# A third quarter's attention outputs kept on the chip: added by GpSimd, with an adding transfer for the first output, and columns in other places of the dense stage

## The chip, the cores and the metric

The kernel runs on one core of one Trainium2 chip. The metric is the device time of one execution in microseconds (us), the median of several runs. The engines are called by their work: TensorE (PE in the profile), VectorE (DVE), ScalarE (ACT), GpSimd (POOL) and SyncE (SP), which only issues transfers here.

## What is computed

One layer of a streaming encoder over 2048 frames of width 1024, in float32: an attention over chunks with a learned position bias, then a dense SwiGLU feed-forward network (FFN), each between two RMS norms and with a residual.

```python
def reference(x, ...):                      # DEPTH is 1, so only mixer 0 runs
    h = rms_norm(x, g_pre_mix)
    m = chunk_relpos_attention(h, w_qkv, w_o, rel_bias)
    x = x + rms_norm(m, g_post_mix)
    h = rms_norm(x, g_pre_ffn)
    return x + rms_norm(swiglu(h, w_gate, w_up, w_down), g_post_ffn)

# chunk_relpos_attention: 16 heads of 64; each chunk c of 64 frames sees chunks max(0, c-8)..c
sc = q_blk @ k[k0:k1].T * scale + bias
out = softmax(sc) @ v[k0:k1]                # all heads side by side, then @ w_o
```

## The kernel before, in words

All activations stand transposed, as 128 partitions by eight column tiles by 512 frames. The 2048 frames are four quarters of 512 frames, and two groups of two quarters. Each float32 operand of a dense product is split in two parts, a high one rounded to fp32r (ScalarE, `split`, L360) and a low one, the rest (VectorE, L361); a product is three matmuls, high by high, high by low and low by high (`products`, L201 to L203). Weights are split in the same way (L136, L137). Many dense products follow Strassen's scheme with seven block products (`B11`, `B21`, `T1`, `T2`, `B22`, `T3`, `T4`), whose operands are sums and differences of blocks; those of the weights that are sums are made by transfers that copy and then add in DRAM (`weight_sums`, L1042 and L1046) or on VectorE (L1109).

The stages follow one another: the projections to queries, keys and values (0 to about 470 us), the attention (to about 1054 us), the dense stage `o_rest` that finishes the output projection of the last two quarters (to about 1110 us), then the FFN, gate and up products and the down product, for each group.

*The attention* goes through the quarters in the order 1, 0, 2, 3 (`SEQ_OF`), so the third quarter in time is quarter 2. A quarter has eight jobs, one for each pair of heads, of four steps each. A step `t` transposes its block of softmax scores on TensorE (L586, into one of a ring of three score banks), lets GpSimd scale the scores of a later step by the inverse row sum (`scaled`, L571), starts the scores of the step three ahead (L542, L543, then VectorE adds the bias in L552 and ScalarE takes the exponential in L557), and fills TensorE's remaining time with dense products of the quarter before (`fill`). When a job ends, `output` multiplies with the values (L622); the result is in a score bank, and ScalarE copies its high part into `ats` (L635), VectorE its low part (L643). For quarter 2 a second copy `at` (L639) goes through a tile of the ring `io` to `at_d` in DRAM. The ring `io` has three tiles, which outputs (`y`), residuals (`res`) and these copies share. For the last quarter only one copy is kept, unsplit (L630).

Dense work during a quarter: `o_quarter` projects the first two quarters' outputs, and during the fourth quarter `o_first` makes the first of the seven block products of the last two quarters, in two halves of four output tiles each. The first half's sum is kept in `p1_d`; the second half's, added to it, is the first four output tiles of quarter 2 in `o_d`. Beside it `Columns` prepares the other operands: it takes quarter 2's attention output back into `at2` (from `at_d`, in two loads), and `t1` (L707) and `others` (L712 to L716) form differences with quarter 3's output. `Late` norms a finished quarter: it loads output and residual, multiplies on VectorE (L1401), adds the residual (L1404, on GpSimd during the attention) and stores `x1`.

*Order.* TensorE's instructions are issued in the order of the program. The other engines' are ordered by a scheduler, by priority and by when it expects them to be ready. Work beside a dense product is put on the list `later`, where each step has a cost; `tick` takes steps off it as TensorE's work is written. The unit is one product of three 512-column matmuls. `timed` places steps at given units, and `pause` waits for some. A name's place (slot) is one of seven tiles `hb0` to `hb6`, which attention outputs, columns, raw loads and terms share one after another; `Blocks` has a list of slots for each group:

```python
self.slot = dict(zip(("B21", "B22", "T3", "T4", "B11", "T1", "T2"), slots))
loads = {"L11": ("T3", 1, 0, 0), "L12": ("T3", 0, 1, 0), "L21": ("T4", 1, 0, 4), "L22": ("T4", 0, 1, 4)}
```

`L11` and the other loads bring blocks of `x1` into the places of T3 and T4; `B11` to `T4` are columns built from them by norm (L877), sum and split. SP's transfers all have line L72, and they are issued in the order of SP's queue.

Of the kernel before, what the change touches and what calls it, by code (L numbers as in the profile page):

```python
# [9 lines left out]
F32 = mybir.dt.float32  # L10
F32R = mybir.dt.float32r  # L11
I32 = mybir.dt.int32  # L12
AF = mybir.ActivationFunctionType
ALU = mybir.AluOpType
# [3 lines left out]
P = 128  # L18
# [5 lines left out]
KT = D // P  # L24
HALF = 512
# [24 lines left out]
def trunk(  # L50
# [45 lines left out]
    y_d = [dram.tile([P, KT, HALF], F32, name=f"y_{i}") for i in range(2)]  # L96

    a_d = [{n: dram.tile([P, NF // 2, HALF], F32, name=f"a{n}_{g}") for n in BLOCKS} for g in range(NG)]
    at_d = dram.tile([P, KT, HALF], F32, name="at")
    p1_d = dram.tile([P, 4, HALF], F32, name="p1")  # L100
    sum_o = {n: [dram.tile([P, 1024], F32, name=f"o_{n}_{c}") for c in range(2)] for n in ("S1", "S2", "S3", "S4")}
    sum_d = {n: dram.tile([NF // 2, P, HALF], F32, name=f"d_{n}") for n in ("S1", "S2", "S3", "S4")}
# [52 lines left out]
    def part_split(c):  # L155
        n = len(ready) - (c > 0)
        if n == len(raws):
            return
        if c == 0:
            ready.append([w_tile(f"{n}_{i}") for i in range(2)])  # L160
        split_part(*ready[n][c], raws[n][c])
# [45 lines left out]
    later = deque()  # L207
# [29 lines left out]
    def pause(w):  # L237
        return [(w, lambda: None)]
# [14 lines left out]
    def io(name):  # L253
        return xp.tile([P, HALF], F32, tag="io", name=name, bufs=3)
# [214 lines left out]
    class Attend:  # L469
# [139 lines left out]
        def output(self):  # L609
            n, p = self.n, self.p  # L610
            v = values[n, p // 2]
            terms = [(0, 4, 0, HALF)]
            for r in range(1, 5 if self.prev else 4):
                if self.prev:
                    terms.append((r, r - 1, 0, r * P))
                if r < 4:
                    terms.append((r, 4 + r, r * P, HALF))
            po = ring[1] if self.alone else self.bank("po")
            for m, (r, kb, c0, c1) in enumerate(terms):
                for h in range(2):  # L620
                    c = (p % 2) * P + h * 64
                    pe.matmul(  # L622
                        po[heads[h], c0:c1], v[:, kb, c : c + 64], self.pT[:, h, r, c0:c1],
                        start=m == 0, stop=m == len(terms) - 1,
                    )
            if n == SEQ_OF[-1]:
                if p == 0:
                    ats[n] = hb_tile(2, F32, (KT, HALF))
                with tc.high_priority(offset=400):
                    act.activation(ats[n][:, p, :], po, AF.Copy)  # L630
                return lambda: None
            if p == 0:
                ats[n] = Cols(((0, 1), (2, 3))[SEQ_OF.index(n) % 2])
            with tc.high_priority(offset=400):
                act.activation(ats[n].hi(p), po, AF.Copy)  # L635
            if n == SEQ_OF[-2]:
                t = io("at")
                with tc.high_priority(offset=400):
                    act.activation(t, po, AF.Copy)  # L639
                sp.dma_start(at_d[:, p, :], t)  # L640
            def low():
                with tc.high_priority(offset=400):
                    dve.tensor_tensor(ats[n].lo(p), po, ats[n].hi(p).bitcast(F32), op=ALU.subtract)  # L643

            return low
# [22 lines left out]
    def o_first(src):  # L668

        for half in range(2):  # L670
            w = take()
            for d in range(4):
                pt = dense_bank(d)
                if half:
                    p1 = io("p1")
                    sp.dma_start(p1, p1_d[:, d, :])
                for k in range(4):
                    hi, lo = w.tiles[d // 2]
                    c = slice(k * 256 + d % 2 * P, k * 256 + d % 2 * P + P)
                    products(pt, hi[:, c], lo[:, c], src.hi(4 * half + k), src.lo(4 * half + k), k == 0, k == 3)  # L680
                    yield 3 * C512
                    if (d, k) == (2, 3):
                        part_split(0)
                    elif (d, k) == (3, 2):
                        part_split(1)
                if half:
                    dve.tensor_tensor(p1, p1, pt, op=ALU.add)
                    sp.dma_start(o_d[SEQ_OF[-2]][:, d, :], p1)
                else:
                    t = io("y")  # L690
                    act.activation(t, pt, AF.Copy)
                    sp.dma_start(p1_d[:, d, :], t)

    class Columns:

# [3 lines left out]
            self.at3 = None  # L699
            self.t = {}  # L700

        def load(self, half):
            here = slice(4 * half, 4 * half + 4)
            sp.dma_start(self.at2[:, here, :], at_d[:, here, :])

        def t1(self, k):
            dve.tensor_tensor(self.at2[:, k, :], ats[SEQ_OF[-1]][:, k, :], self.at2[:, k, :], op=ALU.subtract)  # L707
# [39 lines left out]
            for c, src in enumerate(both)  # L747
        ]

    def o_rest(cols):  # L750

        first, second = SEQ_OF[-2:]
        roots = [bank("prs").rearrange("p (a b) -> p a b", a=4) for _ in range(2)]
# [54 lines left out]
        def put(name):  # L808
            return [(0.8, lambda k=k: cols.put(name, k)) for k in range(4)]

        later.extend(
            put("T2") + put("T4") + [(0.0, begin)] + blocks[0].spreads(lambda name: roots.pop(0))
            + put("T3") + put("B22") + [(0.0, second_terms)]
        )
        slab = take().tiles
        back.ahead(-4)
        yield from product(banks_y, "T1", True, slab, lambda d: None)
        while "two" not in terms:
            later.popleft()[1]()
        banks_x.extend(bank("pd") for _ in range(4))  # L820
        yield from product(banks_x, "T2", True, None, after_t2)
        yield from product(banks_x, "T3", False, None, after_t3)
# [818 lines left out]
    def ffn():  # L1641

        for g in range(NG):
            i = 2 * g
            if g == 0:
                later.extend(pause(12.0))
                for n in (NQ - 2, NQ - 1):
                    later.extend(lates[n].sums(5.0) + lates[n].rstd(1.5) + lates[n].write(10.0))
                later.extend(pause(16.0) + blocks[1].sums(10.0, True))
            else:  # L1650
                for late in halves:
                    later.extend(late.sums(10.0) + late.rstd(1.5) + late.write(14.0))
# [84 lines left out]
    def open_ffn(n):  # L1737
# [2 lines left out]
        phase["psf"] = stack_f[n].enter_context(tc.tile_pool(name=f"psf{n}", bufs=2, space=PSUM, reuse_waits="tile"))  # L1740

    blocks = [
        Blocks([x1_d[2 * g + t] for t in range(2)], PRE_FFN, ((5, 3, 0, 1, 4, 2, 6), (5, 2, 6, 3, 1, 0, 4))[g])
        for g in range(NG)
    ]
    front, items = None, []
# [29 lines left out]
    for c in project():  # L1776
        tick(c / (3 * C512))
        done += c / (3 * C512)
        if 350.0 < done and done % 8.0 < 1.0:
            next(sums_, None)  # L1780
    drain()
    lates = [Late(o_d[n], POST_MIX, x[n], x1_d[n], n) for n in range(NQ)]
# [25 lines left out]
    for t in range(slots):  # L1808
        share = left[0] / max(per - t % per - 1, 1)
        if t > 0 and t % 4 == 0:  # L1810
            fill(0.5 * share)
            low = jobs[t // 4 - 1].output()
            if t % per == 0:
                low()
                low = lambda: None
                n = t // per - 1
                fill(1e9)
                drain()
                work, left[0] = o_quarter(SEQ_OF[n]), KT * KT * 3 * C512
                if n == NQ - 2:  # L1820
                    work, left[0] = o_first(ats[SEQ_OF[n]]), left[0] / 2
                    cols = Columns()
                    cols.load(0)
                if n > 0:
                    late = lates[SEQ_OF[n - 1]]
                    later.extend(pause(5.0) + late.rows(4.0) + late.write(3.0, pool, 1))
                    later.extend(blocks[0].sums(2.0, which=[SEQ_OF[n - 1]]))
        if t == 16:
            fetch()
        elif t in (20, 22):  # L1830
            part_split(t // 2 - 10)
        job = jobs[t // 4]
        if cols is not None:
            s = t % per
            if s == 6:
                cols.load(1)
            if s in (5, 9, 13, 17):
                cols.t1(s // 4 - 1)
            elif s in (18, 19, 22, 23):
                cols.put("T1", (18, 19, 22, 23).index(s))  # L1840
            elif s in (21, 25, 29):
                cols.others(s // 4 - 5, (0,))
            elif s in (26, 27, 30):
                cols.others((26, 27, 30).index(s), (1, 2))
            tick(1.0)
        job.transposed(t % 4)
        job.fifth()
        if t + AHEAD - 1 < slots:
            jobs[(t + AHEAD - 1) // 4].scaled()
        ahead(t + AHEAD)  # L1850
        if t > 0 and t % 4 == 0:
            low()
        fill(share if t % 4 < 3 else 0.5 * share)
# [7 lines left out]

    open_ffn(1)
    first = lambda part, w: blocks[0].build(part, w, lambda t, k, x_: blocks[0].norm(x_, t, k))
    work, done = o_rest(cols), 0.0
    for c in work:
        if done == 0.0:
            later.extend(timed(
                (2.0, first("L11", 0.0)), (2.0, first("L12", 0.0)), (18.0, first("L21", 0.0)), (18.0, first("L22", 0.0)),
                (33.0, first("B11", 2.5)), (49.0, first("B21", 2.5)), (58.0, first("T1", 2.0)),
            ))  # L1870
        tick(c / (3 * C512))
        done += 1.0
    drain()
    later.extend(timed(
        (0.5, first("T2", 3.0)), (13.0, first("B22", 2.0)), (22.0, first("T4", 2.0)), (31.0, first("T3", 1.0)),
# [77 lines left out]
```

## Time and profile before

| What | Value |
|---|---|
| median of 3 runs (lowest to highest) | 2413.51 us (2412.27 to 2416.07) |
| the profiled execution, its own time | 2407.26 us |
| its span, first to last instruction | 2405.5 us |
| TensorE busy | 2321.7 us, 97% of the span |
| VectorE, ScalarE, GpSimd busy | 1673.5, 1146.9, 328.3 us |
| mean granted clock of TensorE | 0.987 |
| transfers | 550.69 MB, mean 229 GB/s |

In a row of the timeline stand the start, the length, the engine, the line, the operation, what it writes and reads, and in brackets the engine's idle time before it with what ended that. In a group (`x58`) stand the summed busy time, the mean of one in ns, and the idle time before them. The tables by stretches have each engine's busy time.

### The profile page before, as it was taken

What the parts mean: (1) busy time and instruction counts of PE and PEld (TensorE: products, weight loads), DVE (VectorE), ACT (ScalarE), POOL (GpSimd) and SP (SyncE); (2) the same over time, 40 slices, a digit from 0 to 9 for tenths busy, and PEclk for the clock granted to TensorE, in tenths of its full rate; (3) what the DMA queues carried; (4) which work ended last, traced back from release to release, by engine and by line L of the source; (5) the groups of instructions that cost most, each with busy time, mean ns of one, the idle gap of its engine ahead of it and who ended that gap; (6) DMA issues with size and microseconds to landing.
All of it is one profiled execution on the core that took longest, in us unless ns stands there. A gap on an engine that the chain in (4) does not pass through costs nothing.

```text
span 2405.5 us, 32939 instructions
## 1 busy us (share of the span) xinstructions
PE 2321.7 (97%) x11388; PEld 1897.5 (79%) x11388; DVE 1673.5 (70%) x2692; ACT 1146.9 (48%) x1995; POOL 328.3 (14%) x432
## 2 busy tenths in 40 slices
PE   9999999989999899799999999999999999999998
PEld 7788888877777687577778788888888888888887
DVE  8787856666665566579869687777657666555577
ACT  7544543367666576455323343365433333334454
POOL 2000011144333434310110000000000000000001
PEclk9999999999999899899999999999999999999999
DMA  8777999998897897865896654477666657447664
GB/s 307 245 259 257 269 324 277 278 253 220 227 252 239 240 258 238 249 243 178 256 294 218 237 193 170 156 242 246 235 203 205 210 156 249 147 148 251 193 192 145
DMA packets 238310, 550.69 MB, mean 229 GB/s; under 512 B 27296, under 2 KB 43696, under 8 KB 233024
## 3 DMA queue, kind: packets, MB, share of 16 engines
q1 hardware_dynamic: 225344, 497.20, 64.8%
q0 software_dynamic: 12800, 51.39, 7.7%
q8 instruction: 90, 1.47, 0.3%
q14 instruction: 76, 0.62, 0.1%
HBM read 397.96 MB, written 181.98 MB: 241 GB/s over the span
## 4 chain that ended last, share of the span: by engine, by line
PE 59%; DMA 6%; DVE 6%; issue 2%; ACT 1%; SPq 1%; POOL 0%; DVEq 0%; POOLq 0%; ACTq 0%
PE pd L201 6%; PE pd L203 6%; PE pd L202 6%; PE pb L201 4%; PE pb L202 4%; PE pb L203 4%; PE pa L202 3%; PE pa L201 3%; PE tt L622 3%; PE pa L203 3%; PE pc L202 3%; PE pc L201 3%; PE pc L203 3%; PE tt L586 2%; PE st L542 2%
## 5 line engine op out<-in xcount | busy, mean ns | idle before, releaser
L571 POOL TENSOR_SCALAR sc<-sc,rows 128x640 f32<-128x640 f32 (+4 forms) x256 | 196.9, 784 | 318.1 <-DVE rows L567 244.6
L557 ACT ACTIVATE sc<-sc,rows 128x640 f32<-128x640 f32 (+4 forms) x256 | 193.2, 757 | 88.6 <-DVE rows L552 87.1
L201 PE MATMUL pb<-hb,w_wg_T 128*128 128x512 f32 x528 | 208.0, 394 | 10.4 <-DVE terms L1217 7.6
L552 DVE CUSTOM_DVE_ANT_0 sc<-st,bias 128x640 f32<-128x640 f32 (+2 forms) x248 | 174.2, 734 | 52.4 <-PE st L543 30.8
L202 PE MATMUL pb<-hb,w_wg_T 128*128 128x512 f32 x528 | 207.5, 393 | 2.9 <-DVE hb L361 2.9
L203 PE MATMUL pb<-hb,w_wg_T 128*128 128x512 f32 x528 | 207.3, 393 | 0.0
L542 PE MATMUL st<-k,q 128*128 128x384 f32 (+3 forms) x432 | 140.9, 343 | 22.4 <-DVE rows L552 13.3
L586 PEld LDWEIGHTS tt<-ident,sc 128*128 128x128 f32 x928 | 107.2, 143 | 52.5 <-POOL sc L571 20.5
L586 PE MATMUL tt<-ident,sc 128*128 128x128 f32 x928 | 128.6, 279 | 19.8 <-DVE hb L643 9.3
L203 PE MATMUL pd<-a,w_d_T 128*128 128x512 f32 (+1 forms) x368 | 139.8, 380 | 0.1
L201 PE MATMUL pd<-a,w_d_T 128*128 128x512 f32 (+1 forms) x368 | 139.9, 380 | 0.0
L202 PE MATMUL pd<-a,w_d_T 128*128 128x512 f32 (+1 forms) x368 | 139.7, 380 | 0.0
L201 PE MATMUL pa<-hb,w_wg_B 128*128 128x512 f32 x352 | 136.9, 389 | 0.0
L202 PE MATMUL pa<-hb,w_wg_B 128*128 128x512 f32 x352 | 136.9, 389 | 0.0
L203 PE MATMUL pa<-hb,w_wg_B 128*128 128x512 f32 x352 | 136.9, 389 | 0.0
L590 DVE COPY pT<-tt 128x512 f32<-128x512 f32 (+3 forms) x128 | 81.7, 638 | 78.4 <-PE tt L586 77.0
L1219 ACT ACTIVATE terms<-terms 128x512 f32<-128x512 f32 x65 | 41.1, 632 | 184.2 <-DVE terms L1217 184.2
L136 ACT ACTIVATE w_wg_T<-raw 128x1024 fp32r<-128x1024 f32 x88 | 93.0, 1058 | 74.7 <-PE pb L203 34.1
L201 PEld LDWEIGHTS pb<-hb,w_wg_T 128*128 128x128 f32 x528 | 100.3, 190 | 34.3 <-issue 9.3
L543 PE MATMUL st<-k,q 128*128 128x384 f32 (+3 forms) x432 | 127.3, 315 | 0.0
L361 DVE TENSOR_TENSOR a<-raw_a,a 128x512 fp32r<-128x512 f32 x154 | 105.4, 693 | 26.3 <-ACT a L360 26.2
L293 POOL TENSOR_TENSOR rs<-ms,neg_half 128x4 f32<-128x4 f32 (+1 forms) x5 | 5.4, 1088 | 850.0 <-DMA raw_a<-aB 813.7
(313 smaller groups left out, 6227.3 us busy)
## 6 DMA issues: line engine op xcount, KB each, us to landing
raw<-in_w_gu SPq DMA_DIRECT2D x77, 512.0 KB, 4.2
q<-q SPq DMA_DIRECT2D x62, 512.0 KB, 6.6
k<-k SPq DMA_DIRECT2D x54, 512.0 KB, 8.8
s_g_S<-raw POOLq DMA_DIRECT2D x44, 512.0 KB, 3.8
raw_a<-aT SPq DMA_DIRECT2D x88, 256.0 KB, 3.6
raw_d<-d_S SPq DMA_DIRECT2D x88, 256.0 KB, 3.7
raw<-s_g_S SPq DMA_DIRECT2D x44, 512.0 KB, 4.0
bias<-ext_d SPq DMA_DIRECT2D x124, 144.0 KB, 8.7
```

Of the source, the lines that this page charges most:

```text
L136: act.activation(hi, raw, AF.Copy)
L201: pe.matmul(pt, a_hi, b_hi, start=first, stop=False, skip_group_check=go_on)
L202: pe.matmul(pt, a_hi, b_lo, start=False, stop=False, skip_group_check=go_on)
L203: pe.matmul(pt, a_lo, b_hi, start=False, stop=last, skip_group_check=go_on)
L361: eng.tensor_tensor(lo, src, hi.bitcast(F32), op=ALU.subtract)
L542: pe.matmul(st[:, a:b], q[:, 2 * h, cols], kk[:, h, key], start=True, stop=False)
L543: pe.matmul(st[:, a:b], q[:, 2 * h + 1, cols], kk[:, h, key], start=False, stop=True)
L552: dve.tensor_tensor_reduce(out=sc[:, :n], in0=st[:, c0 : c0 + n], in1=rev, scale=-1.0, scalar=3.0e38, op0=ALU.add, op1=ALU.min, accum_out= ...
L557: act.activation(sc[:, :n], sc[:, :n], AF.Exp, bias=nmax, scale=-1.0, accum_out=rows[:, h : h + 1])
L571: last_pool[0] = pool.tensor_scalar(sc[:, :n], sc[:, :n], rows[:, 2 + h : 3 + h], 1.0, op0=ALU.mult, op1=ALU.mult)
L586: pe.transpose(tt[:, u, :], sc[h][:, b * P : b * P + P], ident)
L590: dve.tensor_copy(dst, tt[:, : len(part), :])
```

## The change

In the third quarter in time the second copy `at` and its store are gone, and so are `at_d` and the two loads from it. Instead GpSimd adds the high and low parts of that quarter's output into `at2`, one of eight tiles at every second step of the first half of the fourth quarter (`whole`). In `o_first` both halves copy their bank with ScalarE; the first half stores to `p1_d` and to `o_d`, the second half adds to `o_d` by a transfer issued by GpSimd. In `o_rest` the steps are placed at given units together with the loads and columns of the first FFN group, the places of the columns are others, and the loop that ran the remaining steps by force is gone. In the FFN the norms of the last two quarters begin later, and the weight sums begin earlier in the projections.

```diff
             with tc.high_priority(offset=400):
                 act.activation(ats[n].hi(p), po, AF.Copy)
-            if n == SEQ_OF[-2]:
-                t = io("at")
-                with tc.high_priority(offset=400):
-                    act.activation(t, po, AF.Copy)
-                sp.dma_start(at_d[:, p, :], t)
...
                 pt = dense_bank(d)
-                if half:
-                    p1 = io("p1")
-                    sp.dma_start(p1, p1_d[:, d, :])
...
+                t = io("y")
+                act.activation(t, pt, AF.Copy)
                 if half:
-                    dve.tensor_tensor(p1, p1, pt, op=ALU.add)
-                    sp.dma_start(o_d[SEQ_OF[-2]][:, d, :], p1)
+                    last_pool[0] = pool.dma_start(o_d[SEQ_OF[-2]][:, d, :], t, accum_op=ALU.add)
                 else:
-                    t = io("y")
-                    act.activation(t, pt, AF.Copy)
                     sp.dma_start(p1_d[:, d, :], t)
+                    sp.dma_start(o_d[SEQ_OF[-2]][:, d, :], t)
...
-        def load(self, half):
-            here = slice(4 * half, 4 * half + 4)
-            sp.dma_start(self.at2[:, here, :], at_d[:, here, :])
+        def whole(self, k):
+            first = ats[SEQ_OF[-2]]
+            pool.tensor_tensor(self.at2[:, k, :], first.hi(k).bitcast(F32), first.lo(k).bitcast(F32), op=ALU.add)
...
-        later.extend(
-            put("T2") + put("T4") + [(0.0, begin)] + blocks[0].spreads(lambda name: roots.pop(0))
-            + put("T3") + put("B22") + [(0.0, second_terms)]
-        )
+        later.extend(timed(
+            (0.0, put("T2")), (4.0, put("T4")), (8.5, [(0.0, begin)]),
+            (9.0, blocks[0].spreads(lambda name: roots.pop(0))),
+            (12.0, put("T3")), (20.0, put("B22")), (30.0, [(0.0, second_terms)]), *more,
+        ))
...
         yield from product(banks_y, "T1", True, slab, lambda d: None)
-        while "two" not in terms:
-            later.popleft()[1]()
...
-                later.extend(pause(12.0))
+                later.extend(pause(40.0))
                 for n in (NQ - 2, NQ - 1):
-                    later.extend(lates[n].sums(5.0) + lates[n].rstd(1.5) + lates[n].write(10.0))
-                later.extend(pause(16.0) + blocks[1].sums(10.0, True))
+                    later.extend(lates[n].sums(5.0) + lates[n].rstd(1.5) + lates[n].write(12.0))
+                later.extend(pause(8.0) + blocks[1].sums(7.0, True))
...
-        Blocks([x1_d[2 * g + t] for t in range(2)], PRE_FFN, ((5, 3, 0, 1, 4, 2, 6), (5, 2, 6, 3, 1, 0, 4))[g])
+        Blocks([x1_d[2 * g + t] for t in range(2)], PRE_FFN, ((2, 3, 0, 4, 1, 5, 6), (2, 5, 6, 3, 4, 0, 1))[g])
...
-        if 350.0 < done and done % 8.0 < 1.0:
+        if 320.0 < done and done % 8.0 < 1.0:
             next(sums_, None)
...
             s = t % per
-            if s == 6:
-                cols.load(1)
+            if s < 16 and s % 2:
+                cols.whole(s // 2)
...
-                (2.0, first("L11", 0.0)), (2.0, first("L12", 0.0)), (18.0, first("L21", 0.0)), (18.0, first("L22", 0.0)),
-                (33.0, first("B11", 2.5)), (49.0, first("B21", 2.5)), (58.0, first("T1", 2.0)),
...
+        (17.0, first("L11", 0.0)), (17.0, first("L12", 0.0)), (33.0, first("B11", 2.0)),
+        (49.0, first("L21", 0.0)), (49.0, first("L22", 0.0)), (53.0, first("B21", 2.0)), (65.0, first("T1", 2.5)),
```

Before, the second list of `o_rest` was counted from the end of the first one, whose costs sum to 14.8 units.

More of the change, by code (lines that the diff above doesn't have):

```diff
@@ L98, in trunk @@
     a_d = [{n: dram.tile([P, NF // 2, HALF], F32, name=f"a{n}_{g}") for n in BLOCKS} for g in range(NG)]
-    at_d = dram.tile([P, KT, HALF], F32, name="at")
     p1_d = dram.tile([P, 4, HALF], F32, name="p1")
@@ L748, in o_items, with o_rest @@
         ]
-    def o_rest(cols):
+    def o_rest(cols, more):
         first, second = SEQ_OF[-2:]
@@ L1822, in trunk @@
                     cols = Columns()
-                    cols.load(0)
                 if n > 0:
@@ L1863, in trunk @@
     first = lambda part, w: blocks[0].build(part, w, lambda t, k, x_: blocks[0].norm(x_, t, k))
[L1864 to L1867, printed above, removed]
-                (2.0, first("L11", 0.0)), (2.0, first("L12", 0.0)), (18.0, first("L21", 0.0)), (18.0, first("L22", 0.0)),
-                (33.0, first("B11", 2.5)), (49.0, first("B21", 2.5)), (58.0, first("T1", 2.0)),
-            ))
+    for c in o_rest(cols, (
+        (17.0, first("L11", 0.0)), (17.0, first("L12", 0.0)), (33.0, first("B11", 2.0)),
+        (49.0, first("L21", 0.0)), (49.0, first("L22", 0.0)), (53.0, first("B21", 2.0)), (65.0, first("T1", 2.5)),
+    )):
         tick(c / (3 * C512))
-        done += 1.0
     drain()
```

## The prediction, made before the result was known

> **What bounds the kernel now.** I read the page's busy shares first, then a table by stretches, then TensorE's idle times in order of time, each with its releaser.
>
> ```profile
> span 2405.5 us, 32939 instructions
> PE 2321.7 (97%) x11388; PEld 1897.5 (79%) x11388; DVE 1673.5 (70%) x2692; ACT 1146.9 (48%) x1995; POOL 328.3 (14%) x432
> ...
> 740.00:893.00 153.00, 138.98 (x899) 111.12 (x898) 93.10 (x203) 95.37 (x198) 61.09 (x65) 0.94 0.84 249
> 893.00:1057.00 164.00, 143.01 (x929) 109.43 (x928) 103.10 (x228) 97.35 (x204) 61.12 (x68) 0.95 0.78 228
> ...
> 1071.00:1143.00 72.00, 67.39 (x294) 55.28 (x293) 70.94 (x101) 34.77 (x51) 2.80 (x5) 0.98 0.58 206
> ```
>
> The columns after the length are busy time of TensorE, its weight loads, VectorE, ScalarE and GpSimd, then the granted clock, the DMA share and GB/s. TensorE is busy 97% of the span, so a gain can only come out of its idle time, or out of a low clock. The change touches three stretches: the third quarter's attention (740 to 893 us: 14.0 us idle, clock 0.94), the fourth's (893 to 1057: 21.0 us idle, clock 0.95), and the rest of the dense stage with the first FFN products (1071 to 1143: VectorE 70.94 of 72 us busy). The timeline of the third quarter shows where its idle time lies.
>
> ```profile
> 775.83 0.60 ACT L635 ACTIVATE hb<-tt 128x512 fp32r<-128x512 f32 x1 [3.16 <-PE tt L622]
> ...
> 781.09 3.94 POOL L571 TENSOR_SCALAR sc<-sc,rows 128x640 f32<-128x640 f32 x2 [6.18 <-DVE rows L567]
> 781.71 2.74 DVE L137 TENSOR_TENSOR w<-raw,w 128x1024 fp32r<-128x1024 f32 x2
> ...
> 785.00 2.91 POOL L1404 TENSOR_TENSOR y<-res,y 128x512 f32<-128x512 f32 x2
> ...
> 786.72 0.60 ACT L639 ACTIVATE at<-tt 128x512 f32<-128x512 f32 x1 [4.10 <-POOL y L1404]
> ...
> 787.35 0.69 DVE L643 TENSOR_TENSOR hb<-tt,hb 128x512 fp32r<-128x512 f32 x1 [1.78 <-ACT at L639]
> ...
> 788.19 1.94 PE L586 MATMUL tt<-ident,sc 128*128 128x128 f32 x8 [8.82 <-DVE hb L643]
> ```
>
> Read it backwards. TensorE idles 8.82 us before a transpose that needs a score bank; the bank is freed by the low half (L643), which started 0.03 us after the second copy `at` (L639) ended; that copy stood 10 us behind the high half (L635), because its tile of the ring of three `io` tiles was still held by the residual that GpSimd adds in L1404.
>
> ```profile
> 827.15 0.60 ACT L635 ACTIVATE hb<-tt 128x512 fp32r<-128x512 f32 x1 [3.10 <-PE tt L622]
> ...
> 832.42 2.54 POOL L571 TENSOR_SCALAR sc<-sc,rows 128x640 f32<-128x640 f32 x2 [6.39 <-DVE rows L567]
> ...
> 833.03 1.26 DVE L137 TENSOR_TENSOR w<-raw,w 128x1024 fp32r<-128x1024 f32 x1 [0.78 <-ACT w L136]
> 833.38 0.58 ACT L639 ACTIVATE at<-tt 128x512 f32<-128x512 f32 x1
> ...
> 834.21 0.68 DVE L643 TENSOR_TENSOR hb<-tt,hb 128x512 fp32r<-128x512 f32 x1
> ...
> 835.04 1.30 PE L586 MATMUL tt<-ident,sc 128*128 128x128 f32 x5 [4.34 <-POOL sc L571]
> ```
>
> The same two jobs later: 4.34 us idle. The profile names GpSimd, whose scale ended at 834.96; but TensorE starts 0.15 us after the low half's end (834.89), as it did at 788.19 (788.04), so I put this one down to the late low half as well. In the quarter before, which has no `at` copy, the low half follows the high half's end at once (0.03 us here):
>
> ```profile
> 671.47 0.60 ACT L635 ACTIVATE hb<-tt 128x512 fp32r<-128x512 f32 x1 [0.74 <-PE tt L622]
> ...
> 672.10 0.69 DVE L643 TENSOR_TENSOR hb<-tt,hb 128x512 fp32r<-128x512 f32 x1
> ```
>
> **The change, part by part.** *The `at` copies go.* Both idle times above should go: 8.82 + 4.34 us. Behind each the clock is low too:
>
> ```profile
> 780.00:800.00 20.00, 11.81 (x69) 11.14 (x70) 12.02 (x21) 10.42 (x20) 10.84 (x8) 0.74 0.63 174
> 830.00:845.00 15.00, 10.66 (x57) 9.61 (x56) 11.41 (x22) 10.36 (x20) 5.79 (x5) 0.77 0.69 226
> 970.00:985.00 15.00, 7.98 (x32) 6.51 (x32) 6.29 (x15) 5.75 (x12) 2.98 (x4) 0.66 0.81 220
> 1008.00:1020.00 12.00, 8.79 (x41) 4.34 (x42) 6.65 (x11) 5.93 (x11) 4.23 (x4) 0.72 0.80 205
> ```
>
> If the clock is either full or half, 0.74 over 20 us is 10.4 us at half, at least 1.6 us of it beyond the idle 8.8, and work done then loses half: 0.8 us. By the same sum 0.77 over 15 us is 6.9 us, 2.6 beyond the idle 4.3: 1.3 us. What is late next is the bias of a job whose loads were issued just then:
>
> ```profile
> 791.76 2.88 SPq L72 DMA_DIRECT2D bias<-ext_d  x4
> ...
> 811.66 0.42 PE L542 MATMUL st<-k,q 128*128 128x384 f32 x1
> ...
> bias<-ext_d SPq DMA_DIRECT2D x124, 144.0 KB, 8.7
> ```
>
> Issued by 794.6 and landing 8.7 us later, it is there at 803.3; its scores would start at 811.66 - 8.82 = 802.8. I take 1 us back. So -8.6 and -5.6. SP loses eight stores as well, ScalarE eight copies of 0.6 us; both are off the path.
>
> *`Columns.load` becomes `whole`.* Two loads of 1 MB leave SP; GpSimd gets eight adds of 128x512, at every other step of the fourth quarter's first half. Its own add of that shape is the nearest row:
>
> ```profile
> L571 POOL TENSOR_SCALAR sc<-sc,rows 128x640 f32<-128x640 f32 x58 | 48.6, 852 | 72.0 <-DVE rows L567 62.6 <-PE tt L586 5.9 <-PE st L543 3.5
> L1404 POOL TENSOR_TENSOR y<-res,y 128x512 f32<-128x512 f32 x8 | 10.3, 1283 | 16.6 <-DVE y L1401 9.9 <-DVE rows L567 3.9 <-DMA res<-in_x 2.2
> ...
> PEld tt L586 <- POOL sc L571: 4.1, 5, 0.8
> ...
> L1046 POOL DMA_DIRECT2D d_S<-d_S x22: 768/795/1127, 329.9 to 1270.7; - x22
> ```
>
> 8 x 1.28 = 10.3 us on an engine with 61.12 of 164 us busy. Queued behind an add are the scales (L571), for which the transposes wait, and the residual adds (L1404), for whose stores SP waits. The transposes' weight loads waited for scales only 4.1 us in five waits, 0.8 at most, so a scale that is 1.28 us later is nearly always in time. Bounds 0 and 10.3; I take 1, nearest to that row.
>
> The Trainium skill, "SBUF — State Buffer", section "Who interferes with whom", states that a VectorE instruction with two SBUF inputs and a GpSimd instruction that reads SBUF exclude one another for the whole instruction. The row at 781.09 bears it out, two scales in 3.94 us where the mean is 0.85 each. By that rule alone the term would be the upper bound.
>
> *The first outputs.* In the second half of `o_first` a load of `p1`, a VectorE add and an SP store become a ScalarE copy and an adding transfer of GpSimd; the first half gains four SP stores. The removed add was late once:
>
> ```profile
> 1010.47 0.68 DVE L687 TENSOR_TENSOR p<-p,mm 128x512 f32<-128x512 f32 x1
> ...
> 1011.21 0.80 PE L201 MATMUL mm<-hb,w 128*128 128x512 f32 x1 [3.52 <-DVE p L687]
> ```
>
> 3.52 us for a dense bank, and the low clock of 1008 to 1020 (0.72 over 12 us: 6.7 us at half, 3.2 beyond the idle, 1.6 lost): 5.1 us. The ScalarE copy can be late behind exponentials too; I leave 1 us for that: -4.1. Bounds -5.1 and 0. The four adding transfers cost GpSimd some 0.8 us each by L1046; each waits for its copy with scales queued behind it, which are in time as above: 0, at most +3.2. Their landing is awaited only in the FFN.
>
> *The dense stage's order and the places of the columns.* T1 and B11 are built earlier, and L21/L22 are loaded at unit 49 instead of 33. A unit is three matmuls, 3 x 67.39/294 = 0.69 us. VectorE is the bound there: it has 1.1 us to spare in 72, and at the end of that stretch TensorE waits for a column.
>
> ```profile
> 1141.69 0.79 PE L202 MATMUL pb<-hb,w_wg_T 128*128 128x512 f32 x1 [2.94 <-DVE hb L361]
> ...
> hb<-x SPq DMA_DIRECT2D x4, 1024.0 KB, 6.6
> ```
>
> Order alone takes no VectorE work away, so I put it at 0. Bounds: -2.9 if that wait goes; +3.8 if VectorE stands before B21, which is due four units (2.8 us) after a load that lands in 6.6 us. The norms of the last outputs (pause 40 for 12) are the same work 28 units, 19 us, later: 0, and one wait of the size of 1141.69's either way if they meet a full VectorE. The earlier weight sums (320 for 350) are transfers that run behind the projections, each 0.8 us of GpSimd by L1046, and GpSimd's part of them holds nobody up there: 0. The second group's places change no amount and no due time: 0.
>
> Sum: -8.6 - 5.6 - 4.1 + 1 = -17.3. The profiled execution took 2407.26 us, 1.76 over its span, so 2390.0. The runs shown have their median at 2413.51, 6.25 above it (0.26%); on that footing 2396.2. 0.2% (4.8 us) is about what a measurement of this kernel can tell from no change.
>
> **The rivals.** *More goes than counted.* In the fourth quarter SP issues a job's loads behind a store that waits for GpSimd:
>
> ```profile
> 960.67 0.32 SPq L72 DMA_DIRECT2D x<-y  x1
> ...
> 962.07 0.61 SPq L72 DMA_DIRECT2D q<-q  x1
> ...
> 965.45 1.26 SPq L72 DMA_DIRECT2D k<-k  x2
> ...
> 974.90 0.66 PE L542 MATMUL st<-k,q 128*128 128x384 f32 x1 [4.84 <-DMA k<-k]
> ...
> 977.39 0.58 PE L542 MATMUL st<-k,q 128*128 128x256 f32 x1 [1.51 <-DMA k<-k]
> ```
>
> That is 6.35 us idle, and 0.66 over 15 us is 10.2 us at half clock, 3.85 beyond it: 1.9 more. With the loads of `at` and `p1` off SP these 8.3 us may go as well: 2388. Against it, the store ahead of them stays. 20%.
>
> *GpSimd and VectorE block each other.* Each add holds a VectorE operation on the path for its 1.28 us: 10.3 instead of 1, so 2405.5. For it stand the stretched scales of 781.09 and 832.42; against it, that VectorE is busy 103.10 of 164 us there. 12%.
>
> *The change doesn't do what it says.* The low half stays behind the weight split (L137) on VectorE, as the order at 833.03 could also mean. Then only the 1.78 us at 787.35 and the 4.1 go, and 1 comes: -4.9, 2408.6. The row without a copy (672.10) speaks against it. 8%.
>
> *Slower.* The adds delay the residual adds, SP's stores wait for them, and the q and k loads behind those come late for more jobs than the one at 974.90. At 8.3 us each, two more jobs undo the gain and a third makes it slower: -17.3 + 24.9, 2421. 10%, with the late L21 in it.
>
> **How the numbers follow.** My forecast has 50%, by itself 2388 to 2404. Faster: 50 + 20 + 7 of the blocking case's 12 = 77%; within 0.2%: the other 5 and the 8 = 13%; slower 10%. The range goes down into the first rival (8.3 and the 2.9 of the dense stage, some more clock: 2380) and up past the third (2411).
>
> **What would show it.** Right: no `at` rows; every low half within 0.4 us of its high half; no TensorE wait over 3 us between 740 and 893, and that stretch some 14 to 16 us shorter; no wait for a dense bank near 1010. Wrong: a new wait for k or the bias in either quarter, transposes that wait for scales much over 4.1 us, VectorE idle before B21 followed by a longer wait than at 1141.69, or low halves still behind L137.

## The result and the profile after

The changed kernel takes 2393.99 us (median of six runs, 2389.62 to 2397.94), the kernel before 2413.16 in the runs beside it: a ratio of 0.992 (95% interval 0.9905 to 0.9934). Forecast were 2396.2 us, 2380 to 2411. The profiled execution of the changed kernel is its fastest, 2389.62 us. Of one experiment, the first outputs made as before, the profiled execution ran at a granted clock of 0.657; only its other runs are used.

The page's first lines, after:

```profile
span 2387.6 us, 32932 instructions
PE 2319.2 (97%) x11388; PEld 1895.7 (79%) x11388; DVE 1675.7 (70%) x2688; ACT 1143.9 (48%) x1991; POOL 345.2 (14%) x444
```

TensorE has the same work, 17.9 us less span, and GpSimd 16.9 us more to do. For a comparison stage by stage I cut both traces at ScalarE's copies of a job's output: the third quarter from its first job's copy to its last one's, the fourth from there to the last job's. The table by stretches, before:

```profile
736.20:891.70 155.50, 141.48 (x912) 113.31 (x913) 95.15 (x205) 96.64 (x199) 60.92 (x65) 0.95 0.83 247
891.70:1053.80 162.10, 141.11 (x925) 108.11 (x925) 101.26 (x224) 95.46 (x199) 61.30 (x69) 0.95 0.77 223
```

and after:

```profile
738.30:882.20 143.90, 138.83 (x912) 110.36 (x913) 97.37 (x206) 93.62 (x194) 66.08 (x67) 0.99 0.85 249
882.20:1034.90 152.70, 138.38 (x925) 107.05 (x925) 101.10 (x219) 95.58 (x200) 74.69 (x79) 0.98 0.77 222
```

The third quarter is 11.6 us shorter (idle 14.0 to 5.1), the fourth 9.4 (idle 21.0 to 14.3). Before them 2 us are lost, which vary from execution to execution; the dense stage is 55.4 us in both, FFN's first gate and up stage 441.0 and 442.4, and the rest 855. The copies are gone, and at the two places of the prediction the low half (L637 now) starts 0.59 us after the end of the high half (L634), with one copy of transposed scores on VectorE between them:

```profile
777.96 0.60 ACT L634 ACTIVATE hb<-tt 128x512 fp32r<-128x512 f32 x1 [3.15 <-PE tt L621]
779.15 0.68 DVE L637 TENSOR_TENSOR hb<-tt,hb 128x512 fp32r<-128x512 f32 x1
...
818.30 0.60 ACT L634 ACTIVATE hb<-tt 128x512 fp32r<-128x512 f32 x1 [2.81 <-PE tt L621]
819.49 0.68 DVE L637 TENSOR_TENSOR hb<-tt,hb 128x512 fp32r<-128x512 f32 x1
```

In TensorE's timeline these longer waits are left (a dense bank is the bank in which TensorE sums a dense product):

```profile
836.51 0.69 PE L200 MATMUL mm<-hb,w 128*128 128x512 f32 x1 [4.18 <-ACT sq L267]
...
961.70 0.38 PE L541 MATMUL st<-k,q 128*128 128x256 f32 x1 [1.37 <-DMA k<-k]
...
983.86 0.58 PE L541 MATMUL st<-k,q 128*128 128x256 f32 x1 [1.75 <-DMA k<-k]
...
1004.04 0.41 PE L541 MATMUL st<-k,q 128*128 128x384 f32 x1 [1.06 <-DMA k<-k]
1006.20 0.38 PE L541 MATMUL st<-k,q 128*128 128x256 f32 x1 [1.57 <-DMA k<-k]
...
1124.83 0.79 PE L201 MATMUL pb<-hb,w_wg_T 128*128 128x512 f32 x1 [4.12 <-DVE hb L360]
...
1256.34 0.76 PE L200 MATMUL pb<-hb,w_wg_T 128*128 128x512 f32 x1 [5.38 <-DVE terms L1207]
```

The first is new: after the two waits for low halves, a dense bank whose square (taken for the norm of that output) comes late. The long wait for keys (4.84 and 1.51 before) is gone, and four short ones are left. The wait for T3's columns is 1.2 us longer than before.

This execution is the best case of the fourth quarter. Three kernels of the experiments below (other norms, the dense stage as before, FFN work put ahead) have the same instructions as the changed kernel in the last two quarters, in the same order; in their profiled executions the fourth quarter took 157.2, 158.2 and 157.8 us, for 152.7 here and 162.1 before. TensorE's waits for keys in that quarter (in all, times, longest) are, before and in the changed kernel:

```profile
PE st L542 <- DMA k<-k: 8.7, 5, 4.8
```

```profile
PE st L541 <- DMA k<-k: 5.7, 4, 1.7
```

and in those three:

```profile
PE st L541 <- DMA k<-k: 7.0, 5, 2.2
```

```profile
PE st L541 <- DMA k<-k: 7.8, 4, 3.0
```

```profile
PE st L541 <- DMA k<-k: 8.8, 5, 3.4
```

So the one long wait is gone in all four, but the sum of the waits for keys is clearly smaller only in the first.

### The profile page after: what moved, and what is told of

The parts are those of the page before. It is cut to its first block, busy times and chain, and to the rows that moved or that the text cites. A ratio compares the mean times of both kernels' runs of the same rounds, so it can differ in the third digit from the quotient of the medians.

```text
span 2387.6 us, 32932 instructions
## 1 busy us (share of the span) xinstructions
PE 2319.2 (97%) x11388; PEld 1895.7 (79%) x11388; DVE 1675.7 (70%) x2688; ACT 1143.9 (48%) x1991; POOL 345.2 (14%) x444
## 4 chain that ended last, share of the span: by engine, by line
PE 61%; DVE 6%; DMA 5%; ACT 1%; issue 1%; POOL 0%; SPq 0%; DVEq 0%; ACTq 0%
PE pd L200 6%; PE pd L202 6%; PE pd L201 6%; PE pb L201 4%; PE pb L200 4%; PE pb L202 4%; PE tt L621 3%; PE pa L200 3%; PE pa L201 3%; PE pa L202 3%; PE pc L201 3%; PE pc L200 3%; PE pc L202 3%; PE tt L585 2%; PE st L541 2%; PE st L542 2%
## 5 line engine op out<-in xcount | busy, mean ns | idle before, releaser
L570 POOL TENSOR_SCALAR sc<-sc,rows 128x640 f32<-128x640 f32 (+4 forms) x256 | 202.6, 806 | 293.2 <-DVE rows L566 209.2
L541 PE MATMUL st<-k,q 128*128 128x384 f32 (+3 forms) x432 | 140.1, 341 | 20.4 <-DVE rows L551 14.2
```

The lines of the kernel that those rows point to most:

```text
L541: pe.matmul(st[:, a:b], q[:, 2 * h, cols], kk[:, h, key], start=True, stop=False)
L570: last_pool[0] = pool.tensor_scalar(sc[:, :n], sc[:, :n], rows[:, 2 + h : 3 + h], 1.0, op0=ALU.mult, op1=ALU.mult)
```

## The experiments

### The copies alone

The kernel before, with only the copy, its store and its two loads taken out and `whole` put in.

```diff
-            if n == SEQ_OF[-2]:
-                t = io("at")
...
-        def load(self, half):
+        def whole(self, k):
```

> The kernel before with one part of the change alone: the second copy and its transfers are gone, and GpSimd adds the parts (whole). Times are told by four stretches: third quarter (from the copy of its first job's output to that of its last: 155.5 us before, 143.9 after), fourth quarter (to the last copy: 162.1 and 152.7), dense stage (55.5 and 55.5), FFN. My theory: the third quarter's 11.6 us and the fourth's 9.4 come from different parts. This one gives all of the third quarter's (144 us) and leaves the wait for a dense bank near 1010 us in the fourth; the long wait for keys there goes only if the two loads of the copied output had held SP up: then the fourth is near 156, else near 160. Rival: the third quarter's gain is a new order of all engines' queues that only the whole change gives; then the third quarter stays at 150 us or more.

2391.49 us, ratio 0.9914 (0.99 to 0.9927): all that the whole change gives. Third quarter 144.9 us, fourth 155.0. The wait for a dense bank stays, and keys are late behind it:

```profile
992.35 0.50 PE L200 MATMUL mm<-hb,w 128*128 128x512 f32 x1 [3.51 <-DVE p L681]
...
1004.91 0.66 PE L541 MATMUL st<-k,q 128*128 128x384 f32 x1 [2.94 <-DMA k<-k]
1007.28 0.58 PE L541 MATMUL st<-k,q 128*128 128x256 f32 x1 [1.40 <-DMA k<-k]
```

So the gain in both quarters comes with the copies, and with their stores and loads, which this run does not tell apart. At the job that waited 6.35 us for keys 0.70 us is left, although `p1` still goes over SP; at the last job 4.34 us stand where 1.75 stood.

### What made the copy late

The kernel before, copies and all; VectorE adds the residual in the third quarter.

```diff
-late.write(3.0, pool, 1)
+late.write(3.0, dve if n == 1 else pool, 1)
```

> The kernel before with its copies, and one word changed: in the third quarter VectorE, not GpSimd, adds the residual whose tile the copy waits for. If the late low half is a wait for that tile of the io ring, the tile comes free some 4 us sooner at the first place (the add no longer stands behind scales of 3.94 us), so the low half is earlier though the copies are all there: the waits of 8.82 and 4.34 us shrink to 5 and 2 or less, third quarter 148 to 151 us. If the copy itself, or VectorE's order, made the low half late, the waits stay and the quarter is 155 us or longer by VectorE's eight more adds.

2407.16 us (0.998, 0.9971 to 0.9988), third quarter 154.5. The waits are 7.54 and 4.34 us, so my theory missed at both places. At the first, ScalarE still sits idle 1.32 us for the tile before the copy, where it was 4.10. At the second the copy waits for no tile; its timeline:

```profile
828.25 0.60 ACT L635 ACTIVATE hb<-tt 128x512 fp32r<-128x512 f32 x1 [3.14 <-PE tt L622]
...
833.06 1.04 ACT L136 ACTIVATE w<-raw 128x1024 fp32r<-128x1024 f32 x1
...
834.01 0.57 ACT L664 ACTIVATE y<-mm 128x512 f32<-128x512 f32 x1
834.13 1.25 DVE L137 TENSOR_TENSOR w<-raw,w 128x1024 fp32r<-128x1024 f32 x1 [0.78 <-ACT w L136]
834.49 0.58 ACT L639 ACTIVATE at<-tt 128x512 f32<-128x512 f32 x1
...
835.31 0.68 DVE L643 TENSOR_TENSOR hb<-tt,hb 128x512 fp32r<-128x512 f32 x1
```

The copy stands in ScalarE's queue behind two exponentials, a weight split and an output copy, and the low half starts after it, as VectorE's own weight split ends. So here the low half did stand behind a weight split, as my third rival had it; but it moved ahead of it when the copy was taken out. The ring's tile explains at most 4.10 us of the first place, and freeing it sooner took 1.28 us off that wait; the place in the order explains the rest. That the scheduler put the copy there because it expected the tile late is likely, but not shown.

### The first outputs, and the dense stage's order

The changed kernel, once with `o_first` as before, once with the order and the places of the dense stage as before.

```diff
-                    last_pool[0] = pool.dma_start(o_d[SEQ_OF[-2]][:, d, :], t, accum_op=ALU.add)
+                    dve.tensor_tensor(p1, p1, pt, op=ALU.add)
+                    sp.dma_start(o_d[SEQ_OF[-2]][:, d, :], p1)
```

> The changed kernel with the first output tiles made as before (a load of the first part, VectorE's add, a store by SP). My forecast put this part at 4.1 us, all in the fourth quarter: 152.7 becomes 157, with a wait for a dense bank back near 990 to 1010. Rival: the fourth quarter's gain came with SP's freed queue alone; then it stays within 1 us of 152.7.

2393.16 us (0.9916, 0.9902 to 0.993), as the changed kernel: the part is worth nothing that can be measured. Its fourth quarter's length, for which I had set 157 us, is not known.

```diff
-((2, 3, 0, 4, 1, 5, 6), (2, 5, 6, 3, 4, 0, 1))[g])
+((5, 3, 0, 1, 4, 2, 6), (5, 2, 6, 3, 1, 0, 4))[g])
...
+        later.extend(put("T2") + put("T4") + [(0.0, begin)] + ...)
```

> The changed kernel with the dense stage's order and the columns' places as before. My forecast put this part at 0: the dense stage stays at 55.5 us within 0.5, and TensorE's wait for the columns of T3 (2.94 us before, 4.12 after) stays at 3 to 5. Rival: the new order only made up for something that the other parts would have cost; then the stage or that wait grows by 3 us or more.

2391.84 us (0.991, 0.9895 to 0.9925). Dense stage 55.4 us, the wait for T3's columns 2.94 (4.12 in the changed kernel): nothing either.

### The norms of the last quarters

```diff
-                later.extend(pause(40.0))
+                later.extend(pause(12.0))
```

and the other numbers of that list as before, in the changed kernel.

> The changed kernel with the norms of the last two quarters as early and as dense in the FFN as before (pauses of 12 and 16 units, writes at 10, sums at 10). My forecast put this part at 0, with one wait of some 3 us either way: FFN's gate and up stage within 3 us of 442.4, time within 4 us of the changed kernel's. Rival: the later norms are what keeps that stage from being longer; then it is 445 us or more.

2395.73 us (0.9939, 0.9925 to 0.9952), that stage 442.1: nothing. But this run shows something else. Through the attention its instructions are those of the changed kernel in the same order, and its third quarter is as long; yet its fourth:

```profile
882.50:1039.70 157.20, 142.53 (x925) 110.54 (x925) 100.71 (x219) 95.60 (x200) 74.21 (x79) 0.95 0.75 216
```

4.5 us longer with idle time alike (14.7 for 14.3) and the clock at 0.95 instead of 0.98. The last section returns to it.

### GpSimd's adds: twice, and on VectorE

```diff
             pool.tensor_tensor(self.at2[:, k, :], first.hi(k).bitcast(F32), first.lo(k).bitcast(F32), op=ALU.add)
+            pool.tensor_tensor(self.at2[:, k, :], first.hi(k).bitcast(F32), first.lo(k).bitcast(F32), op=ALU.add)
```

> The changed kernel with each of GpSimd's eight adds made twice (the second writes the same tile again), so GpSimd has 10.3 us more at the same places. My theory: the adds lie beside scales that are in time, and cost 1 us or less: the fourth quarter stays within 2 us of 152.7, and the time within 2 us of the changed kernel's. Rival, the blocking of GpSimd and VectorE: as much again as the adds cost now, up to 10.3 us more in the fourth quarter.

2404.41 us (0.997, 0.9958 to 0.9982): 10.4 us more than the changed kernel's 2393.99. My theory missed, and the size is the rival's. The timeline of the fourth quarter's start shows two new waits for scales:

```profile
886.07 2.53 POOL L695 TENSOR_TENSOR hb<-hb 128x512 f32<-128x512 f32 x2
888.56 1.26 POOL L696 TENSOR_TENSOR hb<-hb 128x512 f32<-128x512 f32 x1
889.80 1.57 POOL L570 TENSOR_SCALAR sc<-sc,rows 128x640 f32<-128x640 f32 x2
...
890.65 1.97 PE L585 MATMUL tt<-ident,sc 128*128 128x128 f32 x8 [2.85 <-POOL sc L570]
...
898.61 1.75 PE L585 MATMUL tt<-ident,sc 128*128 128x128 f32 x7 [2.60 <-POOL sc L570]
```

Sixteen adds run nearly one behind another there, none longer than 1.30 us, with scales between them late. So the two waits come from GpSimd's queue; the rest of the 10.4 us is not traced. To see whether eight cost something, VectorE made them:

```diff
-            pool.tensor_tensor(self.at2[:, k, :], first.hi(k)...
+            dve.tensor_tensor(self.at2[:, k, :], first.hi(k)...
```

> The changed kernel with the eight adds on VectorE instead of GpSimd. Doubling them on GpSimd cost 10 us (two waits for scales at the fourth quarter's start). If the single adds already cost a like amount by standing ahead of scales, the fourth quarter becomes shorter than 152.7 by 3 us or more here, although VectorE gets 8 x 0.68 = 5.4 us. If only the second set was too much, it stays within 2 us of 152.7 or grows.

2395.82 us (0.993, 0.9917 to 0.9943), no different from the changed kernel. The fourth quarter took 158.2 us in the profiled execution, like the 157.2 to 158.2 of the three others told above. By itself this could also be two equal costs, as VectorE gets 5.4 us of work. But in the changed kernel TensorE's waits in the two quarters hold none of a matmul for GpSimd. Its adds start like this:

```profile
875.32 5.01 POOL L695 TENSOR_TENSOR hb<-hb 128x512 f32<-128x512 f32 x4 [0.23 <-PE mm L202]
...
879.34 1.54 DVE L268 TENSOR_TENSOR osum<-osum,sq 128x512 f32<-128x512 f32 x1
```

One sum of VectorE took 1.54 us beside them, where the shortest of its kind took 0.67; no wait of TensorE is put down to it. Eight adds on GpSimd cost nothing that can be measured; the second eight cost 10.

### Work put ahead in the order

Three kernels, for the waits that are left: the dense bank's copy and square ahead of other work; T3's columns and each closing sum of the FFN ahead; and both.

```diff
+                with tc.high_priority(offset=400):
                     act.activation(t, pt, AF.Copy)
                     add_square(pt, osums[n], dt == 0)
```

> The changed kernel, with the copy and the square of a dense bank (and the square's sum) put ahead in the order of ScalarE's and VectorE's queues. The third quarter still holds one wait of 4.18 us for a dense bank whose square stood behind two weight splits and two exponentials. Theory: only the order makes it late; the wait goes, with the low clock behind it (3.4 us at half): third quarter 138 to 140 us instead of 143.9, time 4 to 6 us less. Rival: the square is late for want of its scratch tile; then the wait stays, or another takes its place.

```diff
+                with tc.high_priority(offset=400):
...
                     for m in range(4):
                         self.put("T3", m, held[m])
...
+                    with tc.high_priority(offset=400):
                         dve.tensor_tensor(terms[i], pts[i], terms[i], op=op)
```

> The changed kernel, with the columns of T3 and the first operation after each of the last three FFN products put ahead in VectorE's and ScalarE's order. After the change TensorE waits 4.12 us for T3's columns, which stand behind a weight split and a weight sum (2.4 us), and 5.38 us near 1256 behind such ones too. Theory: order alone makes them late, the two waits shrink by 2.4 and 3 us or more, FFN 5 to 9 us shorter (the low clock goes too). Rival: VectorE has no time to spare there (70.94 of 72 us before), so what is put back makes the next product's weights late, and the FFN stays within 2 us.

> The changed kernel with both of these orders. If both theories hold, the gains add: 9 to 15 us less than the changed kernel, 2379 to 2385 us. If VectorE has no time to spare, only the square's 4 to 6 us.

All three are slower than the changed kernel by their medians: 2399.21 (0.9943, 0.9931 to 0.9955), 2399.74 (0.9947, 0.9933 to 0.9961) and 2402.01 us (0.9955, 0.9943 to 0.9967); the intervals of the first two just touch the changed kernel's, so what is sure of them is that they gain nothing. In the first, TensorE's timeline has the wait in two pieces, 2.67 us for 4.18, the second for a weight split that was put back:

```profile
834.20 0.51 PE L200 MATMUL mm<-hb,w 128*128 128x512 f32 x1 [1.59 <-ACT sq L267]
...
836.02 0.80 PE L202 MATMUL mm<-hb,w 128*128 128x512 f32 x1 [1.08 <-DVE w L136]
```

yet its third quarter is 148.2 us. TensorE's waits for VectorE's bias sums are 3.1 us there, for 0.9 in the changed kernel, and 6.8 us are at half clock, for 3.4; the order of many ScalarE and VectorE instructions is another, and which of them did it stays open. In the second, the wait for T3's columns is gone, but one as long follows a product later, and that stage is 450.5 us:

```profile
1175.85 0.77 PE L200 MATMUL pb<-hb,w_wg_T 128*128 128x512 f32 x1 [4.32 <-DVE terms L1209]
```

The stage is 8.1 us longer than in the changed kernel, more than the 2 us of the rival. VectorE is busy without a gap in its first 24.6 us, as the rival said, but only 46.5 of the next 61 us, which hold the new wait; so why the sums are late there is not shown.

### SP's queue

SP's own waits (in all, times, longest) between 738 and 1055 us, before and after:

```profile
SPq L72 <- POOL y L1404: 44.5, 9, 9.7
```

```profile
SPq L72 <- POOL y L1394: 39.1, 9, 7.8
```

A normed row's store stands in SP's queue until GpSimd has added it, with q and k of a later job behind it. In this kernel GpSimd issues these stores itself, after its add:

```diff
                 eng.tensor_tensor(y, res, y, op=ALU.add)
-                sp.dma_start(self.dst[:, dt, :], y)
+                if eng is pool:
+                    last_pool[0] = pool.dma_start(self.dst[:, dt, :], y)
+                else:
+                    sp.dma_start(self.dst[:, dt, :], y)
```

> The changed kernel, with the normed rows' stores during the attention issued by GpSimd's own queue, behind its own add, instead of SP's. What is left of the fourth quarter's waits is mostly keys that land late (1.37, 1.75, 1.06 and 1.57 us after the change; 4.84 and 1.51 before). Theory: SP issues a job's loads late because a store ahead of them in its queue waits for GpSimd's add; without these stores the loads go out earlier, and the waits for keys are under 1 us in all: fourth quarter 146 to 149 us. Rival: the loads go out late because a tile they load into is late, or the transfers are slow (DMA share 0.8 there); then the waits stay at 4 us or more in sum, and 16 issues of some 0.6 us make GpSimd's scales later.

2381.63 us (0.9878, 0.9864 to 0.9891), 12.4 less than the changed kernel. SP has no wait for a GpSimd add left, and two waits for keys (0.88 and 1.75 us) are left, where the theory set under 1 us in all. Table by stretches:

```profile
737.20:875.60 138.40, 137.02 (x912) 109.72 (x913) 98.95 (x206) 93.38 (x195) 68.96 (x75) 1.00 0.87 255
875.60:1022.70 147.10, 136.41 (x925) 106.73 (x924) 100.95 (x219) 95.70 (x200) 77.80 (x87) 0.99 0.82 233
```

The third quarter's 5.5 us are another matter: TensorE waited for no keys there. Its wait for a dense bank (4.18 us) is gone, and with this edit the scheduler gave ScalarE another order there. The square of that bank stood behind two weight splits in the changed kernel (first below) and stands ahead of the second one now:

```profile
831.84 2.00 ACT L135 ACTIVATE w<-raw 128x1024 fp32r<-128x1024 f32 x2
...
835.88 0.58 ACT L267 ACTIVATE sq<-mm 128x512 f32<-128x512 f32 x1
```

```profile
826.96 0.60 ACT L267 ACTIVATE sq<-mm 128x512 f32<-128x512 f32 x1
...
827.96 1.07 ACT L135 ACTIVATE w<-raw 128x1024 fp32r<-128x1024 f32 x1
```

So the loads are shown to come into the fourth quarter's part of the gain alone; the third's came with the order.

Last, the kernel before with these stores, with the copies out and `whole` in, and nothing else of the change:

> The kernel before with two parts alone: no second copy (GpSimd adds the parts), and the normed rows' stores of the attention on GpSimd's queue. The first part alone gave 2391.5 us, the changed kernel 2394.0, the changed kernel with these stores 2381.6. Theory: the first outputs' adding transfer, the dense stage's order, the places and the norms' times are worth nothing between them, and what SP's queue holds up is the same in both: 2378 to 2384 us, third quarter 138 to 140 us. Rival: with the first outputs made as before, SP waits for VectorE's add there instead, and the wait for a dense bank (3.51 us) stays: 2385 us or more.

2380.47 us (0.9864, 0.9843 to 0.9885), 33.1 us under the kernel before beside it. Its median is the lowest of all, though not clear of the last one's. Third quarter 138.4, fourth 147.4. Its wait for a dense bank is there:

```profile
983.34 0.50 PE L200 MATMUL mm<-hb,w 128*128 128x512 f32 x1 [3.51 <-DVE p L681]
```

The fourth quarter is as long as in the kernel above, which has no such wait and two for keys (2.63 us) instead; this one has none for keys.

## Why the prediction was right, point by point

*The copies (-14.2 us).* The sign and the mechanism held: the waits of 8.82 and 4.34 us went, and every low half of the quarter starts 0.6 us after the end of its high half (I had set 0.4). That the wait at 835.04 belonged to the copy and the low half, and not to GpSimd, fits: it went with the copy. The quarter gave 11.6 us, not 14 to 16: what I named as late next, a bias, was not; a dense bank was, 4.18 us and the low clock behind it, so my sign of no wait over 3 us failed. My reason for the late copy, the ring's tile, was the smaller part, and none of it at the second place; with the tile freed sooner the first wait was still 7.54 us. The rest was the copy's place in ScalarE's order.

*GpSimd's adds (+1).* Right in size, not in place: I thought them spread over 16 steps, and all eight started within 12.3 us around the quarter's start. By the rule of the Trainium skill, "SBUF — State Buffer", section "Who interferes with whom", that a VectorE instruction with two SBUF inputs and a GpSimd instruction that reads SBUF shut one another out, the term would have been 10.3 us. The VectorE sum that took 1.54 us beside them (0.67 at the least) agrees with that. But TensorE did not wait for it, each add took 1.29 us, no longer than GpSimd's adds before, and moving them to VectorE changed nothing. What showed as a cost was queueing, from the second set on.

*The first outputs (-4.1).* This term was wrong by its whole size: 2393.16 us without the part, 2393.99 with it. The 3.52 us wait was real and went, but where it goes a wait for keys seems to take its place: the last two kernels differ in it (3.51 us at 983.34 and no wait for keys in the one, 2.63 us for keys in the other) and have the same fourth quarter. They differ in other parts too, so this is likely, not shown. I had priced the wait and not asked what is late next, as I had for the copies.

*The long wait for keys (rival, 20%).* A part of it came: the fourth quarter lost 9.4 us in the profiled execution, and 4.9, 3.9 and 4.3 in the three others with the same order, for a forecast of 3.1. The wait I named went with the copies and their transfers, as the first experiment shows, but waits at the later jobs grew. SP's stores waiting for GpSimd had another part, and the change left that alone: with them on GpSimd's queue the fourth quarter is 147.1 us.

*Dense stage, places, norms, weight sums (0).* Right: order and places, and the norms, undone alone, changed nothing. The weight sums were not tried alone, but the first experiment has none of these parts and takes as long as the changed kernel.

That the sum of -17.3 came out at -17.9 (spans) is in part luck. The third quarter gave 2.6 us less than forecast, and some 3 us were lost outside the two quarters (2.1 before them, 1.4 in FFN's first stage). Against that the fourth gave 6.3 us more in this execution (0.8 to 1.8 in the others), and not from the first outputs, for which I had 4.1. *The rivals:* the low half did not stay behind the weight split, and the slower case did not come.

## What to carry to other kernels

A copy that reads a bank also decides when the bank is free; look at who stands before it in its engine's order, not only at its 0.6 us. A store that waits for another engine, put in a queue of loads, makes the loads late: here it helped to let the engine that finishes the data issue it. Before counting a wait as a gain, name what is late next at that place; and when one thing is put ahead in an engine's order, ask what is put back: here three tries gained nothing. One profiled execution can be the best of several, so compare a stretch over more than one before explaining its length.

## What the runs showed of the hardware

The clock falls without a long idle time. In the run with the early norms, stretches of 3.4 us (busy time of TensorE first, clock after GpSimd):

```profile
959.90:963.30 3.40, 1.58 (x9) 1.29 (x10) 0.78 (x3) 1.50 (x4) 1.58 (x2) 1.00 1.06 286
963.30:966.70 3.40, 3.05 (x12) 2.26 (x10) 2.00 (x4) 0.32 (x1) 0.00 (x0) 0.50 1.05 338
```

and in the changed kernel, with the same instructions:

```profile
959.50:962.90 3.40, 1.79 (x10) 1.46 (x11) 0.86 (x3) 1.57 (x4) 1.57 (x2) 1.00 1.06 298
962.90:966.30 3.40, 2.31 (x17) 1.94 (x16) 2.26 (x5) 1.91 (x4) 0.00 (x0) 1.00 1.04 346
980.00:983.40 3.40, 1.57 (x11) 1.01 (x9) 2.71 (x7) 2.67 (x6) 0.49 (x1) 1.00 1.07 314
983.40:986.80 3.40, 2.94 (x10) 2.55 (x10) 0.83 (x2) 0.02 (x1) 1.07 (x2) 0.51 1.07 289
```

A stretch with 1.57 or 1.58 us of work was followed by half the clock, one with 1.79 was not. The busy time alone doesn't decide it: in the kernel with the dense stage as before, 1.52 us at the wait for the last job's keys were followed by full clock.

```profile
1008.30:1011.70 3.40, 1.52 (x13) 1.23 (x11) 3.40 (x10) 2.55 (x6) 0.40 (x1) 1.00 1.09 300
1011.70:1015.10 3.40, 0.96 (x5) 0.67 (x6) 0.62 (x2) 0.15 (x1) 1.98 (x2) 1.00 1.00 244
```

What does decide stays open. Waits of 1.4 to 2.2 us for keys thus cost half of another 3.4 or 6.8 us, or nothing: in the fourth quarter 6.8 us are at half clock in the changed kernel and 17.0 in the other run, and half of the 10.2 us between them is about the 4.5 us between two executions of the same order. The Trainium skill, "TensorE: Matmul & The Clock Gate", "Part 1: The HAM clock gate", gives a window of 3.4 us that runs freely, with which the low stretches of 3.4 and 6.8 us agree, and the half clock after an idle window; here one that was half idle could be enough, and the measurement decides.
